# A hybrid mixer layer on one core: one 512-column stream for the two parts of an operand, and a fixed issue order for the products

## The chip, the cores and the metric

One core of a Trainium2 chip runs the whole kernel. The metric is the device time of one execution in microseconds; the median of several runs counts. Before the change it is 1409.2 us (three runs, 1405.49 to 1410.98 us).

## What is computed

One layer of a generator over 256 latent tokens and 256 context tokens of width 2048. Everything is float32 outside and is computed to nearly that accuracy inside.

```
mod   = silu(c) @ w_ada + b_ada         six columns of 2048, for latent and context
h     = x * (1 + scale1) + shift1       both streams
p     = h @ w_in                        2048 -> 3600 columns: s5 u, gates u and v, pool p, z, xbc, dt
mix   = concat(S5 scan + GLU, chunked spatial gating, pooling mixer, Mamba-2 SSD)
x1    = layer_norm(alpha * x + gate1 * (mix @ w_out))
h2    = x1 * (1 + scale2) + shift2
g, v  = split(h2 @ w_up)                2048 -> 2 x 5632
out   = layer_norm(alpha * x1 + gate2 * ((gelu(dw_conv3x3(g)) * v) @ w_down))
```

## The kernel before, in words

**Products in two parts.** A float32 weight chunk is split into an upper part `wh` (a ScalarE cast, line 173) and the rest `wl` (a VectorE subtraction, line 174), 512 columns at a time (`split`, `pieces`). The activations are held as two parts as well, in tiles whose second index is the part (`XL`, `mix`, `gR`, `HM`). A product over one k tile of 128 is then three TensorE products into the same 256 columns of a bank, in `mm3` (lines 185 to 187):

```
PE.matmul(o, lhsT=wh, rhs=xh, start=first, stop=False)
PE.matmul(o, lhsT=wh, rhs=xl, start=False, stop=False)
PE.matmul(o, lhsT=wl, rhs=xh, start=False, stop=last)
```

`mm3` serves the single-stream tiles of the second pass (`chan` with `ns == 1`, 10 tiles of 16 k tiles), the output projection (16 x 16), the up product (`half_up`, 86 tiles of 16) and the down product (16 tiles of 44). Where latent and context are both wanted, `mm_two` (line 904) makes six products of 256 columns per k tile. The v and pool columns are made the other way round, with 512 columns of weights as the moving operand (lines 1059 to 1061).

**Modulation.** The modulation columns are vector by matrix products. Columns 0 and 1 are made in the first pass by `gemv_in` (line 879), chunk by chunk of `w_ada`, two column tiles at a time, while the main products of the tiles before run (`first_mm`); each step of the loop over `kp` takes one step of main products and then two chunks. Columns 2 to 4 are made by `gemv` (line 958): for every k, two chunks of 512 KB are loaded, and each serves two products of 32 output rows and 512 columns. The four products of one k go to the four quarters of the rows of one bank; in the trace one such product is two instructions. `tick` takes one step of `gemv` for every 5 us of main product time as the program estimates it. Column 5 is made by VectorE during the up product (`gemv5`, tile `acc`).

**Queues.** All weight chunks go through `load` (line 159), issued by SyncE in program order into a ring of five buffers `raw` (more in the output projection and the up stage); a load waits until the buffer's last reader is done. The four mixers are written as a generator, `side_gen`, whose pieces `pump` puts between the chunks of the main products. The framework simulates the program's timeline when it builds it, and settles the order in which each engine issues its instructions by that and by the program order; nothing ties one product to the next unless data does.

**Stages in the trace.** First pass over the input projection, to about 160 us; second pass and mixers, 160 to 497 us; output projection (`po`), 497 to 609 us; first norm, 609 to 639 us; up (`pu`), 639 to 1137 us; down (`pdn`), 1137 to 1388 us; second norm and stores. In the up stage each pair of tiles (a gate and a value, 44 pairs) has eight convolution steps on VectorE that read the gate's bank, a GELU, and a multiplication that reads the value's bank. `ln_acc` reads the banks of the output projection and of down.

Of the kernel before, what the change touches and what calls it, by code (L numbers as in the profile page):

```python
# [9 lines left out]
F32 = mybir.dt.float32  # L10
# [18 lines left out]
# columns of the packed per-channel parameters  # L29
# [14 lines left out]
# order of the column tiles of the second pass over the input projection  # L44
# [73 lines left out]
def build(tc, A, out, dbg=None):  # L118
# [16 lines left out]
    # accumulators: one bank for the modulation products, the others for the main products and the mixers  # L135
# [90 lines left out]
    # ---------------- constants and parameters  # L226
# [15 lines left out]
    # ---------------- the mixers' tiles  # L242
    # the modulated streams: latent, and context in two parts (column tiles 0 to 11 and the rest)
# [7 lines left out]
    XC = lambda n, k: xc[0][:, n, k] if k < 12 else xc[1][:, n, k - 12]  # L251
    mix = lambda n, k: G_["mix"][0][:, n, k] if k < 12 else G_["mix"][1][:, n, k - 12]
# [7 lines left out]
    def zs(n, shape=None):  # L260
        """A quarter of the scratch tile."""
# [36 lines left out]
    def side_gen():  # L298
        # ---- s5: discretisation
# [9 lines left out]
        def exp_parts(v):  # L309
            """q and s with exp(v) = s + s q, s a power of two, q = expm1 of the rest."""  # L310
# [30 lines left out]
        # sine and cosine minus one of yy: reduced by 2 pi, a quarter of the rest, doubled twice  # L341
# [57 lines left out]
        # powers of a: pn[tau], then in the order that each direction wants them  # L399
# [25 lines left out]
        # pn <- a * pn  # L425
# [6 lines left out]
        # ---- s5: the matrices of a chunk  # L432
# [37 lines left out]
        # ---- s5 u: to (place in chunk, channel) on partitions, through DRAM  # L470
# [3 lines left out]
        # ---- s5: chunk states  # L474
# [16 lines left out]
        # ---- s5: states before each chunk  # L491
# [32 lines left out]
        # within a chunk: the block Toeplitz matrix of both directions, put together by partition moves  # L524
# [72 lines left out]
        # ---- state space duality mixer  # L597
# [8 lines left out]
        # softplus: max(x, 0) + log1p(exp(-|x|)), log1p(e) = 2 atanh(e / (2 + e))  # L606
# [19 lines left out]
        # decay to the end of the chunk (latent) or of the stream (context), by direction and head  # L626
# [3 lines left out]
        # latent: forward wants chunk 0, backward chunk 1  # L630
# [5 lines left out]
        # whole latent chunk  # L636
# [7 lines left out]
        # tokens on partitions: xs and B  # L644
# [730 lines left out]
```

## Time and profile before

| | us |
|---|---|
| median of three runs | 1409.2 |
| lowest and highest run | 1405.49, 1410.98 |
| span of the profiled execution | 1408.3 |
| TensorE busy | 1356.1 |
| VectorE busy | 968.3 |
| ScalarE busy | 620.7 |
| GpSimd busy | 31.5 |

The profiled execution is known by its span, from its first to its last instruction; the median run is 0.9 us longer. Busy means that at least one instruction of the engine was under way. TensorE's products overlap one another, so the length of one says little of its cost: what it costs is the distance from its start to the next start. The granted clock is given as a share of 2.4 GHz. The chain that ended last is followed back from the last instruction, at each step to what released it. A wait is named after what it waited for.

### The profile page before, as it was taken

What the parts mean: (1) busy time and instruction counts of PE and PEld (TensorE: products, weight loads), DVE (VectorE), ACT (ScalarE), POOL (GpSimd) and SP (SyncE); (2) the same over time, 40 slices, a digit from 0 to 9 for tenths busy, and PEclk for the clock granted to TensorE, in tenths of its full rate; (3) what the DMA queues carried; (4) which work ended last, traced back from release to release, by engine and by line L of the source; (5) the groups of instructions that cost most, each with busy time, mean ns of one, the idle gap of its engine ahead of it and who ended that gap; (6) DMA issues with size and microseconds to landing.
All of it is one profiled execution on the core that took longest, in us unless ns stands there. A gap on an engine that the chain in (4) does not pass through costs nothing.

```text
span 1408.3 us, 28249 instructions
## 1 busy us (share of the span) xinstructions
PE 1356.1 (96%) x11176; PEld 1208.5 (86%) x11176; DVE 968.3 (69%) x2016; ACT 620.7 (44%) x1139; POOL 31.5 (2%) x57
## 2 busy tenths in 40 slices
PE   6899899999999999979999999999999999999995
PEld 4688786765567688869999999999999999999995
DVE  8765317786655675567888887888887875555553
ACT  1133331242344544455555554555555554444443
POOL 0000100110010000000000000000000000000001
PEclk9999999999999999989999999999999999999998
DMA  9898744686674479966777776667765656566651
GB/s 359 299 331 315 244 93 153 200 265 217 219 242 141 157 260 321 328 213 197 230 229 233 235 219 211 206 211 225 227 220 165 183 162 202 181 182 190 189 166 60
DMA packets 88324, 305.65 MB, mean 217 GB/s; under 512 B 10376, under 2 KB 12568, under 8 KB 88064
## 3 DMA queue, kind: packets, MB, share of 16 engines
q1 hardware_dynamic: 85552, 295.58, 64.6%
q0 software_dynamic: 2640, 8.28, 2.2%
q8 instruction: 87, 1.43, 0.4%
q14 instruction: 45, 0.37, 0.1%
HBM read 298.02 MB, written 3.67 MB: 214 GB/s over the span
## 4 chain that ended last, share of the span: by engine, by line
PE 88%; DMA 4%; issue 4%; DVE 2%; ACT 1%; POOL 0%; SPq 0%; POOLq 0%; ACTq 0%; DVEq 0%
PE pu L187 12%; PE pu L185 12%; PE pu L186 12%; PE pg L958 6%; PE pdn L187 5%; PE pdn L185 5%; PE pdn L186 5%; PE pA L904 5%; PE bank L904 4%; PE po L185 2%; PE po L186 2%; PE po L187 2%; PE pg L879 2%; PE bank L187 1%; PE bank L186 1%
## 5 line engine op out<-in xcount | busy, mean ns | idle before, releaser
L173 ACT CAST wh<-raw 128x512 fp32r<-128x512 f32 x618 | 380.3, 619 | 476.8 <-PE pu L186 151.5
L174 DVE TENSOR_TENSOR wl<-raw,wh 128x512 fp32r<-128x512 f32 x618 | 422.5, 688 | 243.7 <-ACT wh L173 233.3
L187 PE MATMUL pu<-XL,wl 128*128 128x256 f32 x1376 | 389.9, 283 | 0.0
L185 PE MATMUL pu<-XL,wh 128*128 128x256 f32 x1376 | 389.5, 283 | 0.3 <-DVE cv L199 0.3
L186 PE MATMUL pu<-XL,wh 128*128 128x256 f32 x1376 | 387.5, 282 | 0.0
L185 PEld LDWEIGHTS pu<-XL,wh 128*128 128x128 f32 x1376 | 261.6, 190 | 0.7 <-issue 0.5
L186 PEld LDWEIGHTS pu<-XL,wh 128*128 128x128 f32 x1376 | 261.6, 190 | 0.0
L187 PEld LDWEIGHTS pu<-XL,wl 128*128 128x128 f32 x1376 | 261.5, 190 | 0.0
L199 DVE SCALAR_TENSOR_TENSOR cv<-pu,pc,cv 128x189 f32<-128x189 f32 (+2 forms) x352 | 150.5, 428 | 8.5 <-ACT cv L1262 4.1
L187 PE MATMUL pdn<-gR,wl 128*128 128x256 f32 x448 | 126.5, 282 | 0.0
L185 PE MATMUL pdn<-gR,wh 128*128 128x256 f32 x448 | 126.3, 282 | 0.0
L186 PE MATMUL pdn<-gR,wh 128*128 128x256 f32 x448 | 125.8, 281 | 0.0
L958 PE MATMUL pg<-raw,sc 128*32 128x512 f32 x384 | 105.7, 610 | 3.6 <-DMA raw<-in_wa 3.6
L187 PEld LDWEIGHTS pdn<-gR,wl 128*128 128x128 f32 x448 | 84.7, 189 | 0.0
L185 PEld LDWEIGHTS pdn<-gR,wh 128*128 128x128 f32 x448 | 84.7, 189 | 0.0
L186 PEld LDWEIGHTS pdn<-gR,wh 128*128 128x128 f32 x448 | 84.7, 189 | 0.0
L879 PE MATMUL pg<-raw,sc 128*32 128x128 f32 x976 | 46.4, 301 | 14.1 <-DMA raw<-in_wa 11.9
L199 DVE SCALAR_TENSOR_TENSOR acc<-raw,sc,acc 128x1024 f32<-128x1024 f32 x25 | 32.1, 1285 | 34.4 <-DMA raw<-in_wa 34.4
L185 PE MATMUL po<-mxa,wh 128*128 128x256 f32 x192 | 54.8, 288 | 0.0
L186 PE MATMUL po<-mxa,wh 128*128 128x256 f32 x192 | 54.5, 284 | 0.0
L187 PE MATMUL pdn<-gxa,wl 128*128 128x256 f32 x192 | 54.2, 282 | 0.0
L187 PE MATMUL po<-mxa,wl 128*128 128x256 f32 x192 | 54.1, 283 | 0.0
(352 smaller groups left out, 2361.7 us busy)
## 6 DMA issues: line engine op xcount, KB each, us to landing
raw<-in_wa SPq DMA_DIRECT2D x182, 512.0 KB, 4.8
raw<-in_wu SPq DMA_DIRECT2D x147, 512.0 KB, 4.3
raw<-in_wd SPq DMA_DIRECT2D x80, 512.0 KB, 3.5
raw<-in_w SPq DMA_DIRECT2D x44, 512.0 KB, 4.4
raw<-in_wo SPq DMA_DIRECT2D x32, 512.0 KB, 4.9
rxa<-in_wu SPq DMA_DIRECT2D x29, 512.0 KB, 4.3
w<-in_w SPq DMA_DIRECT2D x16, 384.0 KB, 6.6
Z<-in_xT SPq DMA_DIRECT2D x8, 512.0 KB, 8.6
```

The costliest lines, as they stand in the source:

```text
L173: S.copy(h[:, :n], src)
L174: V.tensor_sub(out=l[:, :n], in0=src, in1=h[:, :n])
L185: PE.matmul(o, lhsT=wh, rhs=xh, start=first, stop=False)
L186: PE.matmul(o, lhsT=wh, rhs=xl, start=False, stop=False)
L187: PE.matmul(o, lhsT=wl, rhs=xh, start=False, stop=last)
L199: V.scalar_tensor_tensor(out=o, in0=a, scalar=s, in1=b, op0=op0, op1=op1)
L879: PE.matmul(pg[32 * j:32 * j + 32, 0:P], lhsT=sc[:, k], rhs=a[:, kk * 512 + j * P:kk * 512 + (j + 1) * P], start=(k == 0), stop=(k == KT - 1))
L904: PE.matmul(pt[:, s * T:(s + 1) * T], lhsT=w[:, c], rhs=x, start=(k == 0 and n == 0 and s == 0 and w is wh), stop=(k == KT - 1 and w is wl ...
L958: PE.matmul(pg[32 * j:32 * j + 32], lhsT=sc[:, k], rhs=a[:, jj * 512:(jj + 1) * 512], start=(k == 0), stop=(k == KT - 1))
```

## The change

Four things are done together.

1. `mm3` makes two products where it made three. The upper part of the weights meets both parts of the operand in one product of 512 columns, which fills both halves of the bank; the rest of the weights meets the upper part of the operand and adds into the first half. The operand is passed as one view with the part as its first free index (`XL[:, :, k]`, `mix2(k)`, `gT2(k)`).
2. Whoever reads such a bank adds its halves: `both` copies the second half to SBUF on ScalarE and adds the first on VectorE (second pass, up); `ln_acc` accumulates twice on VectorE (output projection, down).
3. Every main and modulation product is passed through `chained`, which ties it, without a semaphore, to the one before in the program, so that TensorE issues them in program order. The mixers' products are not tied.
4. `gemv` loads both chunks of a k first and then makes its four products one after another, those of the second chunk first; in the first pass the two chunk steps come ahead of the step of main products.

```
-    def mm3(o, wh, wl, xh, xl, first, last):
-        PE.matmul(o, lhsT=wh, rhs=xh, start=first, stop=False)
-        PE.matmul(o, lhsT=wh, rhs=xl, start=False, stop=False)
-        PE.matmul(o, lhsT=wl, rhs=xh, start=False, stop=last)
+    def mm3(pt, wh, wl, x, first, last):
+        chained(PE.matmul(pt.rearrange("p (n t) -> p n t", n=2), lhsT=wh, rhs=x, start=first, stop=False, skip_group_check=True))
+        chained(PE.matmul(pt[:, :T], lhsT=wl, rhs=x[:, 0], start=False, stop=last, skip_group_check=True))
+
+    def both(pt, t):
+        S.copy(t, pt[:, T:2 * T])
+        tt(t, pt[:, :T], t, AD)
+        return t
...
+    seq = [None]
+
+    def chained(made):
+        ins = made.ins
+        if seq[0] is not None:
+            tc.add_manual_dep(ins, seq[0].name, mybir.DependencyInfo(mybir.DependencyClass.NoSync, mybir.DependencyReason.DATA),
+                              reason="order of the products")
+        seq[0] = ins
...
         for n in range(4):
-            next(f)
             next(g, None)
             next(g, None)
+            next(f)
             pump(P1)
...
         for k in range(KT):
-            for hf in range(2):
-                a = load(A["wa24"][m - 2, k, hf])
-                for jj in range(2):
-                    j = 2 * hf + jj
-                    PE.matmul(pg[32 * j:32 * j + 32], lhsT=sc[:, k], rhs=a[:, jj * 512:(jj + 1) * 512],
-                              start=(k == 0), stop=(k == KT - 1))
+            a = [load(A["wa24"][m - 2, k, hf]) for hf in range(2)]
+            for j in (2, 3, 0, 1):
+                chained(PE.matmul(pg[32 * j:32 * j + 32], lhsT=sc[:, k], rhs=a[j // 2][:, (j % 2) * 512:(j % 2 + 1) * 512],
+                                  start=(k == 0), stop=(k == KT - 1)))
...
                         if ns == 1:
-                            mm3(pt[:, :T], wh[:, c], wl[:, c], XL[:, 0, k], XL[:, 1, k], k == 0, k == KT - 1)
+                            mm3(pt, wh[:, c], wl[:, c], XL[:, :, k], k == 0, k == KT - 1)
...
-        S.activation(out=uT[:, n], in_=pt[:, :T], func=AF.Gelu_apprx_tanh)
+        S.activation(out=uT[:, n], in_=both(pt, uT[:, n]), func=AF.Gelu_apprx_tanh)
...
         stt(d, pt[:, :T], msrc[:, ct:ct + 1], res, MU, AD)
+        stt(d, pt[:, T:2 * T], msrc[:, ct:ct + 1], d, MU, AD)
...
-        pg = ups[2 * f]
+        pg = ups[2 * f] if 2 * f < NUP else both(ups[2 * f], lnp.tile([P, T], F32, tag="lsq", name="both", bufs=2))
```

The value tiles, the z tiles and the last two convolution tiles of the second pass go through `both` in the same way, and the products of lines 879, 904, 958, 1026, 1059 to 1061 and 1212 go through `chained` unchanged. The other lines of the diff drop comments.

## Rows read from the trace of the kernel before

**Rows 1.** The page: busy shares, the chain by engine; then the chain by line

```profile
PE 1356.1 (96%) x11176; PEld 1208.5 (86%) x11176; DVE 968.3 (69%) x2016; ACT 620.7 (44%) x1139; POOL 31.5 (2%) x57
...
PE 88%; DMA 4%; issue 4%; DVE 2%; ACT 1%; POOL 0%; SPq 0%; POOLq 0%; ACTq 0%; DVEq 0%
...
by line: PE pu L187 11.7%; PE pu L185 11.7%; PE pu L186 11.6%; PE pg L958 6.4%; PE pdn L187 4.9%; PE pdn L185 4.8%; PE pdn L186 4.8%; PE pA L904 4.8%; issue 3.8%; PE bank L904 3.7%; PE po L185 2.4%; PE po L186 2.2%; PE po L187 2.2%; PE pg L
```

**Rows 2.** Stages: stretch; length, busy us per engine; granted clock; DMA share; GB/s

```profile
21.00:160.00 139.00, 131.24 (x1682) 110.10 (x1686) 91.57 (x266) 40.07 (x100) 1.09 (x2) 0.98 0.86 310
160.00:497.00 337.00, 328.60 (x2047) 227.28 (x2048) 206.35 (x416) 120.47 (x213) 23.39 (x41) 0.98 0.60 192
497.00:609.00 112.00, 112.00 (x899) 96.20 (x902) 67.44 (x129) 49.19 (x91) 0.00 (x0) 1.00 0.88 308
...
639.00:1137.00 498.00, 497.69 (x4187) 497.09 (x4187) 415.68 (x811) 267.05 (x489) 0.00 (x0) 0.99 0.69 214
1137.00:1388.50 251.50, 250.92 (x2108) 250.67 (x2108) 141.13 (x235) 113.94 (x190) 0.00 (x0) 1.00 0.56 171
```

**Rows 3.** TensorE's queue in order of time: start us, us, line, product, count

```profile
150.73 1.06 PE L958 MATMUL pg<-raw,sc 128*32 128x512 f32 x6
...
211.58 1.04 PE L958 MATMUL pg<-raw,sc 128*32 128x512 f32 x2
212.55 0.38 PE L904 MATMUL bank<-cxb,wh 128*128 128x256 f32 x1
212.87 1.04 PE L958 MATMUL pg<-raw,sc 128*32 128x512 f32 x2
...
520.49 1.06 PE L958 MATMUL pg<-raw,sc 128*32 128x512 f32 x8
521.49 0.38 PE L185 MATMUL po<-mxa,wh 128*128 128x256 f32 x1
...
600.53 1.06 PE L958 MATMUL pg<-raw,sc 128*32 128x512 f32 x8
```

**Rows 4.** Stretches of the down and of the up stage, as rows 2

```profile
1200.00:1250.00 50.00, 50.00 (x422) 50.00 (x422) 28.25 (x47) 23.39 (x39) 0.00 (x0) 1.00 0.61 186
...
880.00:1000.00 120.00, 120.00 (x1012) 120.00 (x1011) 102.81 (x197) 64.17 (x117) 0.00 (x0) 1.00 0.70 217
```

**Rows 5.** TensorE's queue in a run of 512 wide products

```profile
401.22 0.39 PE L1061 MATMUL bank<-wh,XL 128*128 128x512 f32 x1
...
403.26 0.39 PE L1061 MATMUL bank<-wh,XL 128*128 128x512 f32 x1
```

**Rows 6.** Up stage, groups of instructions: count, busy us, mean ns, idle before

```profile
L1277 ACT CAST gR<-cv 128x256 fp32r<-128x256 f32 x28 | 11.4, 405 | 9.3 <-DVE cv L196 9.3
...
L199 DVE SCALAR_TENSOR_TENSOR acc<-raw,sc,acc 128x1024 f32<-128x1024 f32 x9 | 11.6, 1286 | 12.4 <-DMA raw<-in_wa 12.4
L196 DVE TENSOR_TENSOR cv<-cv,pu 128x256 f32<-128x256 f32 x10 | 4.2, 419 | 0.0
L199 DVE SCALAR_TENSOR_TENSOR acc<-rxa,sc,acc 128x1024 f32<-128x1024 f32 x1 | 1.3, 1285 | 0.5 <-DMA rxa<-in_wa 0.5
```

**Rows 7.** TensorE's queue at the end of the mixers

```profile
488.33 0.71 PE L820 MATMUL sg<-wk,vv 128*128 128x128 f32 x4 [1.71 <-ACT tab L788]
```

**Rows 8.** The chain in order of time, second pass

```profile
286.94 9.96 DMA raw<-in_w
```

**Rows 9.** Waits of TensorE and the issue queue: us, times, longest; then DMA issues

```profile
PE pg L879 <- DMA raw<-in_wa: 11.9, 9, 4.9
PE pg L958 <- DMA raw<-in_wa: 3.6, 1, 3.6
...
SPq L159 <- PE pg L958: 193.3, 64, 19.3
...
raw<-in_wa SPq DMA_DIRECT2D x182, 512.0 KB, 4.8
```

More of the change, by code (lines that the diff above doesn't have):

```diff
@@ L251, in build @@
     XC = lambda n, k: xc[0][:, n, k] if k < 12 else xc[1][:, n, k - 12]
+    mix2 = lambda k: G_["mix"][0][:, :, k] if k < 12 else G_["mix"][1][:, :, k - 12]
     mix = lambda n, k: G_["mix"][0][:, n, k] if k < 12 else G_["mix"][1][:, n, k - 12]
@@ L903, in mm_two @@
             for s, x in ((0, XL[:, n, k]), (1, XC(n, k))):
-                PE.matmul(pt[:, s * T:(s + 1) * T], lhsT=w[:, c], rhs=x,
-                          start=(k == 0 and n == 0 and s == 0 and w is wh),
-                          stop=(k == KT - 1 and w is wl and s == 1), skip_group_check=True)
+                chained(PE.matmul(pt[:, s * T:(s + 1) * T], lhsT=w[:, c], rhs=x,
+                                       start=(k == 0 and n == 0 and s == 0 and w is wh),
+                                       stop=(k == KT - 1 and w is wl and s == 1), skip_group_check=True))
     def first_mm(kp, ws):
@@ L953, in gemv @@
         for k in range(KT):
-            for hf in range(2):
-                a = load(A["wa24"][m - 2, k, hf])
-                for jj in range(2):
-                    j = 2 * hf + jj
-                    PE.matmul(pg[32 * j:32 * j + 32], lhsT=sc[:, k], rhs=a[:, jj * 512:(jj + 1) * 512],
-                              start=(k == 0), stop=(k == KT - 1))
+            a = [load(A["wa24"][m - 2, k, hf]) for hf in range(2)]
+            for j in (2, 3, 0, 1):
+                chained(PE.matmul(pg[32 * j:32 * j + 32], lhsT=sc[:, k], rhs=a[j // 2][:, (j % 2) * 512:(j % 2 + 1) * 512],
+                                  start=(k == 0), stop=(k == KT - 1)))
             if k < KT - 1:
@@ L1025, in build @@
             for s, x in ((0, XL[:, n, k]), (1, XC(n, k))):
-                PE.matmul(pdt[:, s * T:(s + 1) * T], lhsT=dp[:, k * 32:k * 32 + P], rhs=x,
-                          start=(k == 0 and n == 0 and s == 0), stop=(k == KT - 1 and n == 1 and s == 1),
-                          skip_group_check=True)
+                chained(PE.matmul(pdt[:, s * T:(s + 1) * T], lhsT=dp[:, k * 32:k * 32 + P], rhs=x,
+                                       start=(k == 0 and n == 0 and s == 0), stop=(k == KT - 1 and n == 1 and s == 1),
+                                       skip_group_check=True))
     pdt2 = bank("pdt2")
@@ L1041, in build @@
         chan(pt, 4 + n, 1)
-        conv1d(6 + n, pt, 1)
+        conv1d(6 + n, both(pt, lnp.tile([P, T], F32, tag="lsq", name="cs", bufs=2)), 1)
     G_["zT"] = M.tile([P, 4, T], F32, tag="q0", name="zT")
@@ L1046, in build @@
         chan(pt, 6 + n, 1)
-        S.activation(out=G_["zT"][:, n], in_=pt[:, :T], func=AF.Silu)
+        S.activation(out=G_["zT"][:, n], in_=both(pt, G_["zT"][:, n]), func=AF.Silu)
     ready.add("z")
@@ L1058, in build @@
                         r = slice(h * P, (h + 1) * P)
-                        PE.matmul(pt[h], lhsT=XL[:, 0, k, r], rhs=wh, start=(k == 0), stop=False)
-                        PE.matmul(pt[h], lhsT=XL[:, 0, k, r], rhs=wl, start=False, stop=False)
-                        PE.matmul(pt[h], lhsT=XL[:, 1, k, r], rhs=wh, start=False, stop=(k == KT - 1))
+                        chained(PE.matmul(pt[h], lhsT=XL[:, 0, k, r], rhs=wh, start=(k == 0), stop=False))
+                        chained(PE.matmul(pt[h], lhsT=XL[:, 0, k, r], rhs=wl, start=False, stop=False))
+                        chained(PE.matmul(pt[h], lhsT=XL[:, 1, k, r], rhs=wh, start=False, stop=(k == KT - 1)))
                 tick(1.3)
@@ L1199, in build @@
     GR = FT - KT
+    gT2 = lambda f: gR[:, :, f] if f < GR else mix2(f - GR)
     gT = lambda n, f: gR[:, n, f] if f < GR else mix(n, f - GR)
@@ L1211, in build @@
             for n in range(NUP):
-                PE.matmul(ups[n][:, :T], lhsT=wr[n][:, kk * P:(kk + 1) * P], rhs=hm[:, k], start=(k == 0),
-                          stop=(k == KT - 1))
+                chained(PE.matmul(ups[n][:, :T], lhsT=wr[n][:, kk * P:(kk + 1) * P], rhs=hm[:, k], start=(k == 0),
+                                       stop=(k == KT - 1)))
     HM = XL
@@ L1225, in half_up @@
                     c = slice(j * P, (j + 1) * P)
-                    mm3(pt[:, :T], wh[:, c], wl[:, c], HM[:, 0, k], HM[:, 1, k], k == 0, k == KT - 1)
+                    mm3(pt, wh[:, c], wl[:, c], HM[:, :, k], k == 0, k == KT - 1)
         return pt
@@ L1274, in build @@
             ups.append(half_up(2 * f + 1))
-        pv = ups[2 * f + 1]
+        pv = ups[2 * f + 1] if 2 * f + 1 < NUP else both(ups[2 * f + 1], lnp.tile([P, T], F32, tag="lsq", name="both", bufs=2))
         tt(o, o, pv[:, :T], MU)
@@ L1299, in build @@
                     c = slice(j * P, (j + 1) * P)
-                    mm3(pt[:, :T], wh[:, c], wl[:, c], gT(0, k), gT(1, k), k == 0, k == FT - 1)
+                    mm3(pt, wh[:, c], wl[:, c], gT2(k), k == 0, k == FT - 1)
                     k += 1
```

4 lines of the change are left out of this document (2 added, 2 removed).

## The prediction

> **What bounds the kernel now.** I read the page's busy shares first, then the chain that ended last, then the span cut by stage, and only then single instructions. TensorE is busy for 96% of the span and carries 88% of the chain, so the path to the end is the queue of products, and time is won only where that queue gets shorter or stands still less [rows 1]. By stage [rows 2] it is fully busy from 497 us to 1388 us (output projection, feed forward up, feed forward down) at a granted clock of 0.99 to 1.00 (the 2.4 GHz level), and busy for 328.6 of 337 us in the second pass over the input projection (160 to 497 us). The first pass (21 to 160 us) is different: TensorE has 131.2 of 139 us, and the DMA share is 0.86. In the output projection the share is 0.88 at 308 GB/s, so a much faster TensorE would meet the transfers there. VectorE holds 83% of the up stage (415.7 of 498 us).
>
> In the chain by line, main products are the largest part, and one smaller line stands out: the modulation product L958 with 6.4%, 90.1 us [rows 1]. How it is spent is seen in the queue itself [rows 3]. Two L958 instructions (one product of 32 output rows) hold TensorE for 0.97 us, from 211.58 to 212.55; eight of them (four products, one for each quarter of the output rows) hold it for 1.00 us, from 520.49 to 521.49. Four quarters issued together cost no more than one alone. Yet in the second pass they mostly come two by two with a main product between. Counted in this view from 150.73 to the last at 600.53 us, the 384 instructions stand in 99 stretches, 58 of them of two; 81 stretches with 224 instructions (28 steps of k) lie in the second pass and take 74.9 us until the next product starts. Each stretch also slows the main products beside it: the one between two stretches takes 0.32 us from its start to the next start (212.55 to 212.87), where the pitch of a long run is 0.12 us [rows 3, 4]; that is 0.2 us a stretch.
>
> **The change, part by part.**
>
> *One stream of 512.* Three products of 256 columns become one of 512 and one of 256 in 2,496 steps (1,376 up, 704 down, 256 output projection, 160 second pass). A long run of 256 has a pitch of 50.00/422 = 118.5 ns [rows 4], so three cost 355.5 ns. A long run of 512, L1059 to L1061, has nine pitches between 401.22 and 403.26, 226.7 ns each [rows 5]. The new step costs 226.7 + 118.5 = 345.2 ns and saves 10.3 ns, in all 25.7 us: 14.2 up, 7.3 down, 2.6 output projection, 1.6 second pass. The bounds: nothing (the moving operand is now two runs of 256 with a gap, which no row shows; if it costs two products' pitch the step stays at 355.5), and 25.7. I take 25.7, since the row is for the same width and type, and correct it by stage below.
>
> The Trainium skill (TensorE: Matmul & The Clock Gate, "Wait — 56ns, not 53.3ns?") gives N/2.4 GHz plus 2.5 ns as the pitch of warm products, and so speaks against this gain: the step would save only those 2.5 ns, an estimate of 6.2 us in all. The rows show 11.8 ns above 256/2.4 and 13.4 ns above 512/2.4, so here the trace does not agree with the page.
>
> *Putting the two halves together.* Each up tile adds a ScalarE copy (0.41 us by the 256 wide cast) and a VectorE add (0.419 us by the 256 wide one) [rows 6]. ScalarE has 267 of 498 us in that stage, so 86 copies, 35 us, hide [rows 2]. VectorE is the question. Between 880 and 1000 us there are 1,012/96 = 10.5 pairs of tiles, 11.39 us each, with VectorE busy 9.75 us of a pair, and idle another 1.22 us in front of each `acc` for a chunk of modulation weights (12.9 us before ten of them) [rows 4, 6]. Two adds make 10.59 us against the new 32 x 345.2 ns = 11.05 us of products. If the whole wait stays, VectorE needs 11.81 us a pair and 34 pairs with that work lose 0.42 us each, 14 us; if it goes, all 43 remaining pairs win the full 0.33 us, 14.2 us. Since the adds fall partly into the time in which the chunk is under way, I leave half the wait: 11.20 us, so 34 x 0.19 + 9 x 0.33 = 9 us won. Down has VectorE at 56% [rows 2], so one more accumulation a tile (0.42 us by the add above) hides, but for the last; 7 us won, and 0.5 us each added to the tails of the output projection and of the kernel. In the second pass ten adds and copies hide beside a VectorE busy 206 of 337 us [rows 2], except behind the last `uT`, where 0.8 us is covered by output products of the other rows.
>
> *One order for the four modulation products.* In the second pass 28 steps of four at 0.99 us instead of 74.9 us win 47.2 us, and 53 stretches fewer at 0.2 us win 10.6: 58 us. Not all of it arrives. First, near the end the mixers themselves set the pace: at 488.33 us TensorE has waited 1.71 us for `tab`, with nothing but a mixer's product `sg` to run [rows 7]; the 17 stretches between 400 and 497 us fill such waits now, so I give back what they would win, about 12.6 us. Second, around 287 us a main chunk is 9.96 us on its way [rows 8], and modulation products ran meanwhile; with a fixed order they can't be pulled forward, 5 us. That is 18 us of new standing still, with bounds of 0 and about 45. So the second pass wins 58 + 1.6 - 18 = 42 us. Three steps that ran ahead before 160 us move to where the program has them, behind the last output products: 3.6 us more there. With the transfers at 0.88 already, I add 2 us, and the output projection loses 3.6 + 2 - 2.6 = 3 us.
>
> *First pass.* There the steps of two chunks now come ahead of the main products, all in a fixed order. Bounds: 19 us won, if the transfers went from a share of 0.86 to all of the 139 us [rows 2], and 12 us lost, if the 11.9 us that TensorE waits for chunks now came a second time [rows 9]. I take 4 us won, 3 of them the three steps that leave: the transfers are nearer to their limit than TensorE's waits are to doubling.
>
> *Sum* against the profiled span of 1408.3 us: -4 - 42 + 3 + 0.5 - 9 - 7 + 0.5 = -58, so 1350.3 us. The median of the runs, 1409.2 us, lies 0.9 us above that span; with it, 1351 us.
>
> **The rivals.**
>
> *The second pass gives most of it back* (40 instead of 18 us): with the modulation products gathered, the mixers' chain of VectorE, ScalarE and small products is what is late next. For it: the wait for `tab`, with the main products used up [rows 7]. Against it: over the stage TensorE stood still for only 8.4 of 337 us [rows 2], so nearly always some product was ready. 1351 + 22 = 1373 us.
>
> *VectorE becomes the bound of the up stage*: 11.8 us a pair, 14 us lost in 34 pairs, 3 us won in the others, so 11 us lost instead of 9 won: 1371 us. For it: 83% busy plus the waits for `acc`; against it: more VectorE work shortens those waits.
>
> *The change doesn't do what it says*: the operand in two runs streams no faster (16 us of the forecast's gain gone), or the mixers' products, which are outside the fixed order, slip between the four (14 of 28 steps broken, 1.18 us each, 16.5 us). Either way 1367 us. The 2.5 ns of the Trainium skill's page on TensorE would act like the first of these, and the chance of that is within this case's.
>
> *Slower: the fixed order makes TensorE stand in front of modulation steps.* A step now needs both its chunks, and all main products stand behind it. A chunk takes 4.8 us from issue to landing, and the issue queue already waits 193.3 us in 64 waits for L958 to free a buffer [rows 9]. If every one of 48 steps waits w, the forecast's 58 us are gone at w = 1.2 us; at half the landing time, 2.4 us, 115 us are lost, 1466 us. Against it: in this queue, in order too, L958 waited for its chunk only once, 3.6 us, and five buffers let chunks be asked for a step ahead.
>
> **How the numbers follow.** The forecast has 0.58, the second pass giving back more 0.14, VectorE as the bound 0.13, the change not doing what it says 0.09, the standing still 0.06. The range runs from 1326 us (no new waits in the second pass, 18 us better, and the full gain up and some of the first pass's, 7) to 1392 us (two of the three milder rivals together, 1387 to 1393); outside lie the slow rival and the case of all three. The milder rivals together would give 1351 + 22 + 20 + 16 = 1409 us, no change. A measurement of this kernel tells about 0.5% from no change. That makes faster 0.90, the same 0.04, slower 0.06.
>
> **What would show it.** L958 in some 48 stretches of eight, and its part of the chain near 48 us; a pitch of about 345 ns for a step of the down stage, which should take some 244 us; VectorE near 95% in the up stage, with TensorE gaps behind `wl` if the second rival holds; TensorE waits for mixer tiles before the output projection if the first holds. TensorE waits for chunks of modulation weights, over 1.2 us a step, would make the prediction wrong.

## The result, and the profile after

The changed kernel takes 1359.9 us (median of four runs, 1357.38 to 1365.92), the kernel before 1410.1 us beside it: a ratio of 0.966, 95% interval 0.9637 to 0.9683. The forecast was 1351 us, in a range of 1326 to 1392. The profiled execution of the changed kernel took 1365.92 us (span 1364.1); its three other spans are 1358.4, 1357.8 and 1355.6 us, so some 6 us of what its rows show belong to that execution, and stage lengths below are good to a few us.

The page after answers to [rows 1]. Busy shares, the chain by engine, the chain by line:

```profile
PE 1291.0 (95%) x8680; PEld 1073.3 (79%) x8680; DVE 1002.9 (74%) x2144; ACT 637.6 (47%) x1234; POOL 31.5 (2%) x57
...
PE 83%; DMA 8%; issue 4%; DVE 3%; ACT 1%; SPq 0%; POOL 0%; POOLq 0%; ACTq 0%; DVEq 0%
PE pu L187 23%; PE pu L188 12%; PE pdn L187 10%; PE pdn L188 5%; PE pA L923 4%; PE po L187 4%; DMA raw<-in_wa 3%; PE bank L923 3%; PE pg L975 3%; DMA raw<-in_w 3%; PE po L188 2%; PE pg L898 2%; PE bank L187 1%; PE pu L1231 1%; PE bank L1077 1%
```

`mm3` is now L187 (512 columns) and L188 (256), the modulation product of the four quarters L975. TensorE has 65 us less to do, L975 is 3% of the chain where L958 was 6.4%, and transfers have gone from 4% to 8% of it. The stages, as in [rows 2], with the boundaries of this execution: first pass, second pass, output projection, up, down.

```profile
21.00:158.00 137.00, 126.89 (x1672) 109.55 (x1672) 90.95 (x265) 40.65 (x99) 1.09 (x2) 0.98 0.83 311
158.00:460.00 302.00, 279.98 (x1869) 212.84 (x1870) 207.13 (x425) 120.35 (x220) 23.40 (x41) 0.95 0.64 210
460.00:574.00 114.00, 111.42 (x650) 81.56 (x649) 73.01 (x146) 49.32 (x93) 0.00 (x0) 1.00 0.86 313
607.50:1097.20 489.70, 489.36 (x2819) 427.26 (x2818) 438.28 (x894) 284.99 (x574) 0.00 (x0) 1.00 0.65 217
1097.20:1345.70 248.50, 247.31 (x1412) 216.05 (x1411) 146.16 (x253) 112.71 (x191) 0.00 (x0) 1.00 0.56 173
```

The second pass carries the result. TensorE is busy 48.6 us less in it (328.60 before) and idle 22.0 us instead of 8.4, so the stage is 35 us shorter. From the first and last product of each stage (up from its first f32 product):

| us | before | forecast | after | difference, forecast and measured |
|---|---|---|---|---|
| first pass, its end | 159.7 | 155.7 | 157.7 | -4, -2.0 |
| second pass | 336.9 | 294.9 | 302.1 | -42, -34.8 |
| output projection | 110.7 | 113.7 | 114.4 | +3, +3.7 |
| norm | 15.3 | 15.8 | 17.2 | +0.5, +1.9 |
| up | 514.9 | 505.9 | 505.8 | -9, -9.1 |
| down | 252.4 | 245.4 | 248.4 | -7, -4.0 |
| tail | 18.4 | 18.9 | 18.5 | +0.5, +0.1 |
| span | 1408.3 | 1350.3 | 1364.1 | -58, -44.2 |

In *adjacent*, *dve_more* and *grouped* (below), which leave the second pass's order and chunks as they are, it took 296.9 to 297.6 us, so some 5 of the 302.1 us belong to this execution.

In the queue, as in [rows 3], a modulation step of the second pass is now one stretch:

```profile
211.87 1.07 PE L975 MATMUL pg<-raw,sc 128*32 128x512 f32 x8
212.86 0.38 PE L923 MATMUL bank<-XL,wh 128*128 128x256 f32 x1
...
218.81 1.07 PE L975 MATMUL pg<-raw,sc 128*32 128x512 f32 x8
219.80 0.38 PE L923 MATMUL bank<-XL,wh 128*128 128x256 f32 x1
```

Eight instructions hold TensorE for 0.99 us. In the second pass there are now 29 steps (232 instructions, one step more than before) in 34 stretches, 26 of them of eight; they take 34.9 us until the next product starts. Before, 28 steps lay in 81 stretches and took 74.9 us.

What stands still in their place is seen in the waits of the second pass (us in all, times, longest), in TensorE's queue and clock, in the chain, and in the issue queue:

```profile
ACT wh L173 <- DMA raw<-in_w: 90.0, 22, 19.0
...
PE bank L923 <- DVE XB L206: 6.4, 1, 6.4
PE rms L805 <- DVE vals L203: 5.7, 2, 2.9
PE pg L975 <- DMA raw<-in_wa: 3.4, 3, 2.9
PE bank L923 <- ACT wh L173: 2.6, 1, 2.6
```
```profile
164.29 0.55 PE L923 MATMUL bank<-XL,wh 128*128 128x256 f32 x1 [6.35 <-DVE XB L206]
164.64 0.41 PE L923 MATMUL bank<-cxa,wh 128*128 128x256 f32 x1
164.85 0.41 PE L923 MATMUL bank<-XL,wh 128*128 128x256 f32 x1
```
```profile
163.20:169.60 6.40, 5.31 (x24) 5.20 (x24) 0.90 (x2) 0.85 (x2) 1.88 (x3) 0.50 0.47 159
```
```profile
171.31 12.44 DMA raw<-in_w
...
269.22 11.48 DMA raw<-in_w
```
```profile
161.41 9.80 SPq L159 DMA_DIRECT2D raw<-in_wa  x2
171.31 0.38 SPq L159 DMA_DIRECT2D raw<-in_w  x1
```
```profile
SPq L159 <- PE pg L975: 9.1, 1, 9.1
```

TensorE's longest wait, 6.4 us, is for no chunk. After the last product of the first pass, at 158 us, the next main product goes into a bank that VectorE still reads for a mixer (`XB`). In the kernel before, TensorE ran 18 instructions of modulation there, from 159.92 us on, and waited 3.6 us for a chunk; in the tied order no modulation product may go ahead. From 163 us, in the wait, to 170 us the granted clock is 0.50 (the 1.2 GHz level), and the main products behind it start 0.21 us apart, where it is 0.12 at a clock of 1.00.

This wait goes on into the issue queue. Of the two modulation chunks in the row above one goes out at 161.41 us; the other waits 9.1 us for the buffer of a modulation step that stands behind those main products. The main chunk behind them is asked for only at 171.31 us and then takes 12.44 us, beside a mixer's transfers on GpSimd's queue. ScalarE, which makes the upper part of the main weights, waits 90.0 us for main chunks in this stage, 32.2 us before. That alone doesn't say that chunks come later: before, it waited another 98 us for TensorE to free buffers of split weights, now 18, and the issue queue waits less for modulation steps than it did (89.1 us, before 170.6). From 171 to 184 us the two queues took (packets, MB, share of the 16 engines' time):

```profile
q1 hardware_dynamic: 473, 1.75, 60.5%
q0 software_dynamic: 268, 0.70, 40.9%
```

Main and modulation chunks share five buffers. Where TensorE's 22.0 us of idle time lie, and its clock at the end of the mixers:

```profile
158.00:200.00 42.00, 33.07 (x254) 29.77 (x255) 10.16 (x15) 15.55 (x35) 6.09 (x10) 0.92 0.63 160
...
250.00:300.00 50.00, 43.89 (x263) 30.21 (x263) 43.51 (x108) 21.55 (x41) 5.16 (x11) 0.97 0.85 274
...
430.00:440.00 10.00, 10.00 (x52) 8.11 (x52) 4.27 (x8) 3.09 (x5) 0.00 (x0) 0.69 0.00 1
440.00:445.00 5.00, 4.30 (x26) 3.37 (x22) 4.44 (x10) 1.62 (x5) 0.55 (x1) 1.00 0.14 52
445.00:450.00 5.00, 1.19 (x2) 0.50 (x2) 3.62 (x7) 2.33 (x4) 0.00 (x0) 0.64 0.28 105
450.00:455.00 5.00, 3.80 (x16) 3.65 (x17) 4.72 (x9) 1.27 (x3) 0.00 (x0) 0.50 0.00 0
455.00:460.00 5.00, 4.02 (x21) 3.40 (x21) 3.79 (x10) 1.85 (x5) 0.00 (x0) 0.83 0.02 3
```

15.0 us lie in the first two stretches: 6.3 us in front of the bank, 2.9 us in front of a modulation chunk at 276 us, and 5 to 6 us in front of main weights, the longest of these 2.65 us behind the chunk of 171.31 us. Another 6.7 us lie in the last 20 us of the stage, where TensorE waits for the mixers (`vals`). There the granted clock is down to 0.50 (the 1.2 GHz level) from 450 to 455 us; it was 0.69 on average already from 430 to 440 us, where TensorE was busy throughout and nothing was transferred. In all of the stage TensorE is busy 26.0 us at a granted clock of 0.50, before the change 10.2 us.

### The profile page after: what moved, and what is told of

The parts are those of the page before. It is cut to its first block, busy times and chain, and to the rows that moved or that the text cites. A ratio compares the mean times of both kernels' runs of the same rounds, so it can differ in the third digit from the quotient of the medians.

```text
span 1364.1 us, 23556 instructions
## 1 busy us (share of the span) xinstructions
PE 1291.0 (95%) x8680; PEld 1073.3 (79%) x8680; DVE 1002.9 (74%) x2144; ACT 637.6 (47%) x1234; POOL 31.5 (2%) x57
## 4 chain that ended last, share of the span: by engine, by line
PE 83%; DMA 8%; issue 4%; DVE 3%; ACT 1%; SPq 0%; POOL 0%; POOLq 0%; ACTq 0%; DVEq 0%
PE pu L187 23%; PE pu L188 12%; PE pdn L187 10%; PE pdn L188 5%; PE pA L923 4%; PE po L187 4%; DMA raw<-in_wa 3%; PE bank L923 3%; PE pg L975 3%; DMA raw<-in_w 3%; PE po L188 2%; PE pg L898 2%; PE bank L187 1%; PE pu L1231 1%; PE bank L1077 1%
## 5 line engine op out<-in xcount | busy, mean ns | idle before, releaser
L187 PE MATMUL pu<-XL,wh 128*128 128x512 f32 x1376 | 485.0, 396 | 0.3 <-DVE cv L206 0.3
L188 PE MATMUL pu<-XL,wl 128*128 128x256 f32 x1376 | 386.9, 281 | 0.0
L187 PEld LDWEIGHTS pu<-XL,wh 128*128 128x128 f32 x1376 | 259.1, 188 | 61.6 <-issue 0.6
L188 PEld LDWEIGHTS pu<-XL,wl 128*128 128x128 f32 x1376 | 260.4, 189 | 0.0
L187 PE MATMUL pdn<-gR,wh 128*128 128x512 f32 x448 | 157.9, 395 | 0.0
L206 DVE SCALAR_TENSOR_TENSOR cv<-both,pc,cv 128x189 f32<-128x189 f32 (+2 forms) x344 | 146.7, 426 | 3.5 <-ACT cv L1281 1.3
L188 PE MATMUL pdn<-gR,wl 128*128 128x256 f32 x448 | 125.7, 281 | 0.0
L187 PEld LDWEIGHTS pdn<-gR,wh 128*128 128x128 f32 x448 | 84.1, 188 | 19.7
L188 PEld LDWEIGHTS pdn<-gR,wl 128*128 128x128 f32 x448 | 84.5, 189 | 0.0
L187 PE MATMUL po<-mxa,wh 128*128 128x512 f32 x192 | 69.9, 404 | 0.9 <-DVE mxa L613 0.9
L187 PE MATMUL pdn<-gxa,wh 128*128 128x512 f32 x192 | 67.9, 394 | 0.0
L187 PE MATMUL bank<-XL,wh 128*128 128x512 f32 x160 | 60.7, 416 | 1.1 <-ACT wh L173 1.1
L975 PE MATMUL pg<-raw,sc 128*32 128x512 f32 x384 | 55.3, 614 | 3.4 <-DMA raw<-in_wa 3.4
L923 PE MATMUL pA<-XL,wh 128*128 128x256 f32 x192 | 55.9, 310 | 0.0
L188 PE MATMUL pdn<-gxa,wl 128*128 128x256 f32 x192 | 53.8, 280 | 0.0
L188 PE MATMUL po<-mxa,wl 128*128 128x256 f32 x192 | 53.6, 279 | 0.0
L187 PEld LDWEIGHTS po<-mxa,wh 128*128 128x128 f32 x192 | 36.0, 188 | 17.3 <-ACT wh L173 5.9
```

Of the source, the lines that this page charges most:

```text
L187: chained(PE.matmul(pt.rearrange("p (n t) -> p n t", n=2), lhsT=wh, rhs=x, start=first, stop=False, skip_group_check=True))
L188: chained(PE.matmul(pt[:, :T], lhsT=wl, rhs=x[:, 0], start=False, stop=last, skip_group_check=True))
L206: V.scalar_tensor_tensor(out=o, in0=a, scalar=s, in1=b, op0=op0, op1=op1)
L923: chained(PE.matmul(pt[:, s * T:(s + 1) * T], lhsT=w[:, c], rhs=x, start=(k == 0 and n == 0 and s == 0 and w is wh), stop=(k == KT - 1 and ...
L975: chained(PE.matmul(pg[32 * j:32 * j + 32], lhsT=sc[:, k], rhs=a[j // 2][:, (j % 2) * 512:(j % 2 + 1) * 512], start=(k == 0), stop=(k == K ...
```

## The experiments

All are edits of the changed kernel, and all ratios are against the kernel before. The stage lengths come from one profiled execution each.

| kernel | median us | ratio, 95% interval | second pass | up | down |
|---|---|---|---|---|---|
| the change | 1359.9 | 0.966 (0.9637 to 0.9683) | 302.1 | 505.8 | 248.4 |
| stream_only | 1405.0 | 0.9985 (0.9964 to 1.0005) | 334.8 | 509.9 | 248.4 |
| order_only | 1377.6 | 0.9786 (0.9764 to 0.9808) | 299.2 | 515.3 | 252.3 |
| no_chain | 1388.9 | 0.9868 (0.9839 to 0.9897) | 330.0 | 505.1 | 248.4 |
| chain_pairs | 1358.8 | 0.9653 (0.9629 to 0.9677) | 293.3 | 505.8 | 248.4 |
| adjacent | 1359.2 | 0.9638 (0.9609 to 0.9667) | 297.1 | 504.3 | 248.5 |
| dve_more | 1392.4 | 0.9893 (0.9851 to 0.9935) | 297.6 | 537.8 | 248.4 |
| gstep | 1365.5 | 0.9688 (0.9656 to 0.972) | 306.8 | 505.4 | 248.4 |
| raw6 | 1345.5 | 0.9541 (0.9515 to 0.9566) | 289.9 | 505.9 | 248.4 |
| w3 | 1359.9 | 0.9656 (0.963 to 0.9682) | 296.5 | 510.4 | 248.4 |
| raw6_gstep | 1350.6 | 0.9593 (0.9565 to 0.9621) | 295.6 | 505.6 | 248.4 |
| grouped | 1356.2 | 0.9636 (0.9602 to 0.967) | 296.9 | 501.3 | 247.5 |
| raw6_grouped | 1339.6 | 0.9495 (0.9474 to 0.9516) | 290.8 | 502.9 | 247.5 |

**The two parts alone.** *stream_only* takes back the order: `chained` ties nothing, the first pass and `gemv` are as before.

```
-        if seq[0] is not None:
-            tc.add_manual_dep(ins, seq[0].name, ...)
-        seq[0] = ins
+        return made
...
-            a = [load(A["wa24"][m - 2, k, hf]) for hf in range(2)]
-            for j in (2, 3, 0, 1):
...
+            for hf in range(2):
+                a = load(A["wa24"][m - 2, k, hf])
```

> Only the 512-column stream and the adding of the halves; products in the order of before (no fixed order, modulation loads and products as before). Theory (two thirds or more of the 50 us come from the order, the stream gives some 13 us: 9 in the up stage, 3 in down, 1 to 2 elsewhere): about 1397 us, modulation products still in some 100 stretches. Rival (the stream is the main part, 25 us by the 10.3 ns of a step, and the order gives most of its gain back in waits): about 1385 us.

Both missed: 1405.0 us, and the interval holds 1. The stream did save 5.0 us up and 4.0 down. But in the output projection (6.2 us longer than before) and the norm (3.0 us longer) it went again: without the tie the modulation products of the output projection lie in 20 stretches that take 22.3 us, before in 16 with 17.7 us. In the second pass they are about as broken as before, 232 instructions in 82 stretches that take 77.0 us. Why the output projection breaks them up more is not shown.

*order_only* keeps the order and takes back the stream (three products of 256, `both` and the second accumulation of `ln_acc` gone).

```
-        chained(PE.matmul(pt.rearrange("p (n t) -> p n t", n=2), lhsT=wh, rhs=x, ...))
-        chained(PE.matmul(pt[:, :T], lhsT=wl, rhs=x[:, 0], ...))
+        chained(PE.matmul(pt[:, :T], lhsT=wh, rhs=x[:, 0], start=first, stop=False))
+        chained(PE.matmul(pt[:, :T], lhsT=wh, rhs=x[:, 1], start=False, stop=False))
+        chained(PE.matmul(pt[:, :T], lhsT=wl, rhs=x[:, 0], start=False, stop=last))
```

> Three products of 256 columns per step as before, no halves to add; the fixed order, the four modulation products together and the new order of the first pass as in the change. Theory: some 50 stretches of modulation products, about 1373 us, with the standing still of the second pass as in the changed kernel. Rival (the stream is the main part): about 1385 us. If the two parts hinder each other (a faster stream only exposes the second pass's waits), this alone reaches 1365 us.

The time lies between the two expectations, nearer the theory. The order alone gives 30 us or so (0.9786): the second pass is 38 us shorter (299.2 us, 232 instructions in 35 stretches), the output projection and the norm some 7 us longer. The stream on top of it is worth 1377.6 - 1359.9 = 18 us; without the order it is worth 2 us, which is not told from nothing.

**Which piece of the order.** *no_chain* takes back only the tie (the first three lines of stream_only's diff); *chain_pairs* keeps the tie and takes back only `gemv`'s two loads first and its order of the quarters.

> The changed kernel without the tie between products: both chunks of a step are still loaded first and its four products written together. As built, the modulation products stand in 81 stretches instead of 50. Theory (the tie makes the stretches): 31 stretches more at 1.18 us cost 37 us, and up to 14 us of new standing still go away, so 1375 to 1397 us. Rival (the loads and the place of the four products in the program are enough): within 5 us of 1360 us.

> The changed kernel, but each chunk of a modulation step is loaded just ahead of its own two products, first chunk first, as before; the tie stays. As built, the products stand in 49 stretches as in the changed kernel. Theory (the tie alone matters): 1356 to 1366 us. Rival (the last chunk must come first, so that TensorE doesn't stop between the two pairs): some 0.5 us at each of 48 steps, about 1384 us.

Both theories held: it is the tie that gathers the steps. Without it the second pass is back at 330.0 us, with 62 stretches for 29 steps, though the program names the four products one after another. In that kernel's queue (L971 is the modulation product, L919 a main one) they still mostly come two by two:

```profile
204.85 1.04 PE L971 MATMUL pg<-raw,sc 128*32 128x512 f32 x2
205.83 0.39 PE L919 MATMUL bank<-cxb,wh 128*128 128x256 f32 x1
206.14 1.04 PE L971 MATMUL pg<-raw,sc 128*32 128x512 f32 x2
207.12 0.38 PE L919 MATMUL bank<-XL,wh 128*128 128x256 f32 x1
```

From one pair to the next are 206.14 - 204.85 = 1.29 us, so four quarters take 5.16 us with four main products among them, where the tied step takes 0.99 us and four main products in a run another 0.5. With the tie and the old loads, 1358.8 us is not told from the change's 1359.9: which chunk is loaded first, and the order of the quarters, are worth nothing here. Without the tie they, or the new order of the first pass, are worth something: *stream_only* lacks all of it, *no_chain* the tie alone, and the two are 16 us apart (1405.0 and 1388.9). No run tells these two edits apart, and none takes the first pass's order out of a tied kernel.

**The pitch of a step.** The forecast had 345.2 ns. The down and the up stage of the changed kernel, as [rows 4]:

```profile
1200.00:1250.00 50.00, 50.00 (x288) 43.70 (x287) 28.89 (x49) 23.28 (x39) 0.00 (x0) 1.00 0.60 184
850.00:970.00 120.00, 120.00 (x687) 104.86 (x686) 108.55 (x218) 68.43 (x139) 0.00 (x0) 1.00 0.66 220
```

Counted like the forecast's 118.5 ns, 287 or 288 products in 50 us make some 347.8 ns a step, 2.6 ns more than forecast. But such a count takes in the products that are under way at the edges of the stretch: 687 in 120 us make 349.3. From start to start it comes out without that:

```profile
1199.64 0.40 PE L187 MATMUL pdn<-gR,wh 128*128 128x512 f32 x1
...
1201.74 0.39 PE L187 MATMUL pdn<-gxa,wh 128*128 128x512 f32 x1
```

Six steps in 2.10 us are 350 ns each. Over the two stretches above it is 350.4 and 350.7 ns; in the kernel before, the three products took 356.8 and 356.7 ns in the stretches of [rows 4], 118.9 ns each. So the step saves 6.0 to 6.4 ns, and it lies 4.8 ns above 226.7 + 118.9 = 345.6 ns. The expectations below still have the counted 347.8 and 2.6 ns.

*adjacent* asks whether the gap between the two parts of the operand costs the difference: it lays them side by side.

```
-    XL = base.tile([P, 2, KT, T], F32R, name="XL")
+    XL = base.tile([P, KT, 2, T], F32R, name="XL")
...
-    gR = fp.tile([P, 2, FT - KT, T], F32R, name="gR", bufs=1)
+    gR = fp.tile([P, FT - KT, 2, T], F32R, name="gR", bufs=1)
```

> The changed kernel with the two parts of an operand side by side in memory (XL and gR as k, part, token), so that the 512 columns are one run; the operands in the mixer tiles stay in two runs. Theory (the step costs 347.8 ns and not the 345.2 of the forecast because wide and narrow products take turns, whatever the operand's layout): pitch of a step of the down stage over gR within 1 ns of 347.8, time within 3 us of 1360. Rival (the gap between the two runs costs the 2.6 ns): 345.2 ns a step over XL and gR, some 5 us less.

The same two stretches of that kernel:

```profile
1200.00:1250.00 50.00, 50.00 (x287) 43.72 (x286) 30.24 (x53) 23.59 (x40) 0.00 (x0) 1.00 0.64 186
850.00:970.00 120.00, 120.00 (x687) 104.86 (x686) 108.71 (x219) 69.05 (x141) 0.00 (x0) 1.00 0.70 223
```

The same counts, and 350.4 and 350.6 ns from start to start: a gap in the moving operand costs nothing that these rows show. *grouped* asks whether the alternation does:

```
-                for j in range(4):
-                    c = slice(j * P, (j + 1) * P)
-                    mm3(pt, wh[:, c], wl[:, c], gT2(k), k == 0, k == FT - 1)
-                    k += 1
+                mm12(pt, wh, wl, [gT2(k + j) for j in range(4)], k, FT)
+                k += 4
...
+    def mm12(pt, wh, wl, xs, k, K):
+        for j, x in enumerate(xs):
+            chained(PE.matmul(pt.rearrange("p (n t) -> p n t", n=2), lhsT=wh[:, j * P:(j + 1) * P], rhs=x, ...))
+        for j, x in enumerate(xs):
+            chained(PE.matmul(pt[:, :T], lhsT=wl[:, j * P:(j + 1) * P], rhs=x[:, 0], ...))
```

> The changed kernel with the products of four steps of a half tile grouped in the up and down stages: four products of 512 columns with wh, then four of 256 with wl, instead of alternating 512 and 256. Nothing is left out; the sums are made in another order. Theory (the 2.6 to 3 ns by which a step takes longer than 226.7 + 118.5 = 345.2 ns come from the alternation, each 256 column product standing behind a 512 column one and in front of one): the pitch of four steps in the down stage falls from 4 x 348 to 4 x 345.5 ns, down gets 1.7 us shorter and up 3.4 us, together 1354 to 1357 us. Rival (the length of a step is set by something that both orders share, such as a weight load for every product beside it): 50 us of the down stage still hold 287 or 288 products, up and down stay within 1 us of 505.8 and 248.4 us, 1359 to 1361 us.

Its down stage, and the starts of groups of four, 20 steps apart:

```profile
1170.00:1220.00 50.00, 50.00 (x289) 43.88 (x288) 29.19 (x48) 23.46 (x39) 0.00 (x0) 1.00 0.65 192
1220.00:1270.00 50.00, 50.00 (x289) 43.86 (x288) 29.30 (x48) 23.33 (x40) 0.00 (x0) 1.00 0.63 184
```
```profile
1195.93 1.09 PE L192 MATMUL pdn<-gR,wh 128*128 128x512 f32 x4
...
1202.91 1.08 PE L192 MATMUL pdn<-gR,wh 128*128 128x512 f32 x4
```

A step takes 6.98 us / 20 = 349 ns in down and, from start to start between 850 and 970 us, 346.3 ns in up. So the alternation accounts for most of the 4.8 ns in up, and in down for 1 to 2 of them; what holds the rest there is open. The stages tell it too: up 4.5 us shorter (3.3 ns a step), down 0.9 (1.3 ns a step, where 1.7 us were expected). The time, 1356.2 us, is as the theory had it, but is not told apart from the change's by the intervals.

**Is VectorE at its limit in the up stage?** *dve_more* adds one operation of VectorE, 0.42 us, behind each `both` of that stage; it changes no value.

```
+    def both2(pt, t):
+        both(pt, t)
+        tt(t, t, t, ALU.max)
+        return t
```

> The changed kernel with one more VectorE operation of 256 columns (0.42 us, the tile with itself, values unchanged) behind each adding of halves in the up stage, 84 to 86 in all. A pair of tiles has 9.8 us of VectorE work and 0.95 us of waits for modulation chunks in 11.15 us of products. Theory (the waits shrink when VectorE has more to do, so it is not the bound and has room for one more): up stage up to 3 us longer, about 1361 us. Rival (the waits stay and VectorE is at its limit): 11.6 us a pair in 34 pairs, 14 us longer, about 1374 us.

Up grew by 32 us, more than either expected: 0.37 us of the 0.42 for each of the 86 tiles. TensorE's waits in that stage, VectorE's, and one of the stretches that suffer:

```profile
PE pu L187 <- DVE both L208: 22.2, 13, 3.7
```
```profile
DVE wl L174 <- ACT wh L173: 26.2, 67, 1.5
DVE acc L211 <- DMA raw<-in_wa: 20.3, 20, 2.3
DVE acc L211 <- DMA rxa<-in_wa: 1.6, 5, 0.7
```
```profile
880.00:920.00 40.00, 36.87 (x209) 31.83 (x208) 36.49 (x75) 21.27 (x42) 0.00 (x0) 1.00 0.56 184
```

So VectorE at 91% is as good as full: 22 us of its waits for `acc` stay even then, and 26.2 us of waits for ScalarE's `wh`. TensorE's waits make 22.2 of the 32 us; the rest is not divided up here. In the changed kernel VectorE's waits for `acc` are

```profile
DVE acc L206 <- DMA raw<-in_wa: 23.4, 20, 1.8
...
DVE acc L206 <- DMA rxa<-in_wa: 6.0, 5, 1.5
```

29.4 us (41.3 before). From 850 to 970 us VectorE is busy 108.55 us and idle 9.5 + 0.8 us in front of `acc`: 118.9 of 120. It just does not hold TensorE up, which waits for VectorE 0.3 us in the whole stage. One more operation tips it over.

**What the order costs in the second pass.** *gstep* has the planner count a modulation step at 4.6 instead of 5.0 us; *raw6* gives the chunks six buffers instead of five, and makes room by three instead of four for the split weights; *w3* makes the room only.

```
-GSTEP = 5.0
+GSTEP = 4.6
```
```
-RAW_BUFS = 5
-W_BUFS = 4
+RAW_BUFS = 6
+W_BUFS = 3
```

> The changed kernel with a modulation step for every 4.6 us of main product time instead of 5.0, so that none trail behind the last output products (three do now). Theory (the trailing steps and their chunks hold up the first chunks of the up stage): from the last output product to the first split up product 15 us instead of 17, about 1358 us. Rival (the second pass and the output projection have no room for more chunks, at a DMA share of 0.86 in the latter): what is won there is lost before, within 1 us of 1360, or slower.

> The changed kernel with six weight chunk buffers instead of five, paid for with three pairs of split buffers instead of four. Theory (TensorE stands still in the second pass since main chunks are asked for only when a buffer comes free, and then land 11 to 12 us later beside the mixers' small packets): the second pass shorter by 5 to 14 us, 1346 to 1355 us. Rival (the chunks are late by contention alone, or the split buffers were needed): no gain, or slower by the waits for split buffers, 1360 us or more.

> The changed kernel with three buffers instead of four for each part of the split weights, and five for the chunks as they come: the half of the run with six chunk buffers that made room for the other half. Theory (the sixth chunk buffer, asked for earlier, won that run's 12 us in the second pass and 4 us in the first): with W_BUFS 3 alone the second pass stays at 302 us or gets longer by up to 5 us, the first pass at 157 to 160 us, and the time is 1358 to 1367 us. Rival (fewer split buffers were the gain, since the splits then run less far ahead and the chunks keep the order in which TensorE wants them): the second pass falls to about 290 us and the time to 1343 to 1348 us.

The smaller step made the norm 6 us shorter (10.9 us) and the second pass 5 us longer: no gain, as the rival had it. The sixth buffer gave 14 us, a little more than the theory's range: 1342.3 to 1346.48 us against 1357.38 to 1365.92, and w3, which lacks only that buffer, has 1358.87 to 1361.9. In w3's profile the second pass lies between the two expectations (296.5 us, as in *adjacent*, *dve_more* and *grouped*) and up is 4.6 us longer, with 4.1 us in nine waits of TensorE for `wl`; the time is the change's. ScalarE's wait for main chunks in raw6's second pass, and in w3's:

```profile
ACT wh L173 <- DMA raw<-in_w: 45.5, 12, 11.2
```
```profile
ACT wh L173 <- DMA raw<-in_w: 61.5, 19, 12.0
```

Of the 90.0 us, which are 70.1 to 83.6 in *adjacent*, *dve_more* and *grouped*, w3 has 61.5 and raw6 45.5. Beside w3, TensorE idles 16.5 us instead of 18.8 in raw6's second pass, and 28 of the 29 modulation steps there stand in stretches of eight, 25 in w3; the wait for the bank stays (5.0 us, 5.2 in w3). The profiled second pass is 6.6 us shorter than w3's, up 4.5 and the first pass 3.6 us.

**Together.** *raw6_gstep* and *raw6_grouped* put gstep's and grouped's edit on raw6.

> Six chunk buffers, three split buffers (as in the run of that name, 1345 us) and the planner's modulation step at 4.6 instead of 5.0 us. Alone, the smaller step shortened the norm from 17.2 to 10.9 us and cost 5 us in the second pass. Theory (those 5 us were TensorE standing in front of modulation steps whose chunks found no free buffer, so a sixth buffer takes most of them away): second pass 290 to 292 us, norm 9 to 12 us, time 1340 to 1344 us. Rival (the 5 us are modulation work moved forward in front of main products that the mixers then miss, whatever the buffers): second pass 294 to 297 us, time 1344 to 1349 us, no gain over the run with six buffers alone.

> Six chunk buffers with three split buffers, and the products of four steps grouped in the up and down stages: the two edits of this study that each gave time, together. Theory (they act on different stages and add): second pass about 290 us as with six buffers, up about 501 and down about 247.5 us as with the grouping, so 1345.5 - 4 to 5 = 1340 to 1342 us. Rival (with grouping, TensorE is done with no wh before four products of 512 and holds all four steps' wl until the end, so three split buffers instead of four are now what it waits for): up back at 506 to 512 us, 1346 to 1352 us, no better than six buffers alone.

The smaller step costs 5 us with six buffers as well (1350.6 against 1345.5 us, and their runs do not overlap), so it is not a matter of the sixth buffer. That modulation steps moved forward stand before main products that the mixers want fits this, but no row here shows it; and the norm is hardly shorter this time (13.8 us, in raw6 14.1). Buffers and grouping add by their medians: 1339.6 us, ratio 0.9495, the fastest here and faster than the kernel before and the change; up is at 502.9 and the second pass at 290.8 us. The runs with and without the grouping (1338.26 to 1343.89 us, 1342.3 to 1346.48) overlap a little. That TensorE would wait for `wl` with three split buffers did not come here (1.5 us in three waits).

## Why the prediction was right, and where not

Right: it is faster, by gathering the modulation steps, and the time lies in the range, 9 us above the forecast. Step by step:

- *One order for the modulation products* (58 us won, 18 given back). That the tie gathers the steps is shown by no_chain and chain_pairs. The sizes: TensorE's busy time fell by 48.6 us, where 58 + 1.6 were forecast. Of the missing 11 us, 1 is the 29th step, which had run in the first pass, and about 2 are three steps that mixers' products, which are not tied, still break up (the third rival had 14). For most of the rest the clock is a candidate, for which the sum has no term: 15.8 us more at a granted clock of 0.50, where main products start 0.21 instead of 0.12 us apart, make an estimate of 7 us; no run here sets the clock apart.
- *New standing still* (18 us: 12.6 at the mixers' end, 5 for a late main chunk). Measured 22.0 - 8.4 = 13.6 us, a fair size from other terms, which is luck. At the mixers' end TensorE idles 6.7 us where it was 2.2, so 4.5. In front of main weights it stands 5 to 6 us, about 2.4 before. The largest wait is one that the sum lacks: 6.4 us for a bank that VectorE reads at the start of the stage, where untied kernels run modulation products; order_only and chain_pairs have it too (6.7 and 6.2 us), no_chain and stream_only don't. So the forecast's reason, that modulation work can't be pulled forward, holds, in another place than it named. TensorE itself stood before modulation steps for 3.4 us only, so the rival that the change is slower fell. But the sentence against it, "five buffers let chunks be asked for a step ahead", was too sure: a sixth was worth 14 us (raw6, w3).
- *One stream of 512* (345.2 ns a step, a gain of 10.3 ns). From start to start it is 350.4 ns, and 356.8 before, a gain of 6.4 ns in down and 6.0 in up. The rows for 512 and 256 were from runs of their own, and taking turns costs more (grouped). Over 1,376 steps that makes 8.3 us, over 704 4.5, where 14.2 and 7.3 were forecast. The rival that the operand in two runs streams no faster fell (adjacent, and every down stage). The Trainium skill (TensorE: Matmul & The Clock Gate, "Wait — 56ns, not 53.3ns?"), by which a saved product is worth 2.5 ns, is again not borne out: it is worth 6.0 to 6.4 ns here.
- *Up* (9 us won). 9.1 measured, but by other terms, so the agreement is luck: the step wins 8.3 us where 14.2 less VectorE's part were forecast, TensorE's wait among the first f32 products is 0.9 us shorter, and VectorE takes nothing. Its waits for `acc` did not fall to half, but from 41.3 to 29.4 us; yet its busy time grew less than two adds a pair, to 108.55/10.73 = 10.11 us (9.75 before, 10.59 forecast), since its operations overlap more: their lengths sum to 11.50 us a pair, 10.80 before. Busy time and waits for `acc` make 11.07 us a pair, just under TensorE's 32 x 350.7 ns = 11.22. The rival with VectorE as the bound fell for this kernel, by a narrow margin (dve_more).
- *Down* (7 us won). 4.0: 4.5 from the step, less 0.6 us by which TensorE's longest wait, for `dT` after a tile, grew (1.2 us, before 0.6).
- *Output projection* (+3): +3.7, partly by other terms. Of the three steps that ran ahead, two (2 us) now stand among the output products and one in the second pass. Three steps trail behind the output products, as they did before: the last modulation products of the trace before start at 607.47 us, not, as the prediction reads, at 600.53. Another 2.6 us are new standing still (busy 111.42 of 114 us, before 112.00 of 112).
- *First pass* (-4): -2.0, right in kind. In the first pass, too, the fixed order waits for chunks: it ends at 154.0 us without the tie and at 153.8 with six buffers.
- *The norm* (+0.5): +1.9. In gstep, where no modulation step trails behind the output products, it is 6 us shorter.

The first rival, 40 us given back in the second pass, fell too: of 59.6 us the stage kept 34.8, so 25 were lost, busy and idle time together, and some 20 by the stage's length in adjacent, dve_more and grouped. What the sum missed besides is that its parts are not independent. The stream was counted at 25.7 us of product time whatever the order; with the order it brought 18 us, without it 2.

## What to carry to other kernels

Small products that could share the array gain only if the issue order keeps them together, and writing them one after another does not ensure it: look in the queue, and tie them. With a fixed order an engine stands in front of whatever comes next, a bank or a chunk, and nothing fills in; so after such a change read its waits one by one, and count the buffers that the loads share. Here one more buffer was worth 14 us beside the change's 50. A pitch is taken from start to start, not from a count over a stretch. When an engine off the path is busy for 90% of a stage, add its waits for data before calling the rest slack.

## What the runs showed of the hardware

- Two L971 instructions (one quarter of the output rows) hold TensorE 0.98 us, eight (four quarters) 0.99. The Trainium skill (TensorEngine Tiling (Array Packing), "Key Properties") says that tiles can work in parallel; the rows agree when the four stand next to one another, and show nothing of it when a main product of all columns stands between.
- A product of 512 columns that alternates with one of 256 makes a step of 350.4 ns; in groups of four it is 346.3 in up and 349 in down, and the sum of the two pitches in runs of their own 345.6.
- A main chunk of 512 KB took 12.44 us to land beside transfers that took 40.9% of the engines' time for 0.70 MB; before the change the median was 4.8 us for modulation chunks of the same size [rows 9]. No run sets apart what made it late.
- Saving 6 ns in a step won nothing (0.9985) as long as the order was loose: the output projection, where modulation products broke into 20 stretches instead of 16, and the norm took it back.
